# Moving the pools in SBUF by 192 bytes, so that the main matmul operands begin at multiples of 512 bytes

## The chip, the cores and the metric

The kernel runs on one core of one Trainium2 chip. The metric is the device time of one execution in microseconds. A trace by the hardware profiler shows one profiled execution; its span runs from the first to the last instruction of the program.

## What is computed

A trunk of four layers over x with 256 tokens of 1024 channels, float32. Each layer has a token mixer and then a SwiGLU network (FFN); after each of the two there is a residual sum and a layer norm. Cut to what matters:

```python
for i in range(4):
    kind = i % 3
    if kind == 0:   h = _hgrn2_mixer(x, ...)   # x @ w_in (1024 x 4096), gated recurrence, @ w_out (1024 x 1024)
    elif kind == 1: h = _mlstm_mixer(x, ...)   # x @ w_in (1024 x 3088), matrix memory, @ w_out (1024 x 1024)
    else:           h = _s5_mixer(x, ...)      # x @ w_in (1024 x 1024), state space, @ w_out (1024 x 2048)
    x = _layernorm(ALPHA * x + h, ...)
    x = _layernorm(ALPHA * x + _swiglu(x, w_gate_up[i], w_down[i]), ...)

def _swiglu(x, w_gate_up, w_down):             # 1024 x 5632 and 2816 x 1024
    gate, up = jnp.split(x @ w_gate_up, 2, axis=-1)
    return (jax.nn.silu(gate) * up) @ w_down
```

Layers 0 and 3 have the HGRN mixer, layer 1 the mLSTM mixer, layer 2 the S5 mixer.

## The kernel before

**Products in three parts.** The large products run on TensorE in the type float32r, in one pass. To keep float32's accuracy, each operand is split in two: hi, a copy of it in float32r, and lo, the rest. A product is then three matmuls, hi by hi, lo by hi and hi by lo, which add up in one bank of PSUM (`mm3`, L180 to L182).

**Weights.** They come from HBM in units of 128 partitions x 2048 float32 (1 MB). `fetch` (L101) loads a unit into a tile w of the pool `stage`, which has three buffers. `stage_next` (L112) splits each half of it into a pair of tiles hi and lo of 128 x 1024: ScalarE copies w to hi (L149), VectorE subtracts (L150). The pool `split` has 8 buffers for hi and 8 for lo. A plan (`plan`, L1361) gives the order of the units; `wstage` takes a unit and stages up to one unit ahead (`AHEAD`). SyncE (SP) issues the transfers, in the order that the scheduler gives them.

**The activation.** x is kept transposed and split in the tile xx, 128 partitions x 8 x 2 x 256: for each of eight blocks of channels, 256 tokens of the high part (`xh`) and 256 of the low one (`xl`). The layer norm writes it by way of TensorE's transposes (L271), which use the identity in the tile ident, and `put_split` (L290 and L291).

**Who is moving, who is stationary.** In a matmul the stationary operand (128 x 128, 512 bytes for each partition) is loaded first; the moving operand streams past it.
- `as_part` (L184): xx is stationary, the weights' hi and lo move, 512 columns. The rows of the profile are named g<-hi,xx and a<-hi,xx: output, moving, stationary.
- `ws_block` (L197): the weights are stationary, xx moves, 256 columns (g<-xx,hi).
- `ws_wide` (L205), in the FFN: hi stationary with xh and xl together moving, 512 columns (L210), and lo stationary with xh moving, 256 columns (L213).
- The FFN's second product: the hidden values, split in tiles hh and hl of 128 x 256, are stationary, the weights move, 512 columns (a<-hi,hh). The output projection of the mixers has the tiles oh and ol in the same role.

**The FFN's order.** For each block of 256 hidden channels: `across` makes the gate and the up values (L350 and L351 add the two halves of a bank), `parts` splits their product into hh and hl (L339, L340), `dproj` multiplies the block before.

**Memory.** SBUF is given out per partition, pool after pool and tile after tile, in the order in which they are made, each tile rounded up to 32 bytes. What the runtime and the framework keep ends at byte 16512 (32 times 512 and 128 more). Then follow the pool `const` (ident 512 bytes, root 32, eps 4, xx 16384, and later the two hnw of 4 bytes and lb of 64), `stage` (3 x 8192), `split` (16 x 4096), `xp` (3 x 4096), `gbp` (8192) and `small` (1216 in all). Every pool that a layer opens for itself lies behind these. In layer 0 and layer 1 the FFN's pool stands behind other tiles that live through it, those of the S5 preparation; those are at their place until the S5 mixer of layer 2 has ended.

**The small tiles.** root holds -0.5, for the powers on GpSimd (POOL) in `rsqrt` (L223). eps is the bias of one square root at the end. lb holds the lower bounds of the HGRN gates, written once in layer 1 (L480, L481) and read by ScalarE in layer 3. hnw0 and hnw1 are the norm weights of the two HGRN layers, loaded by SP (L589).

Of the kernel before, what the change touches and what calls it, by code (L numbers as in the profile page):

```python
# [9 lines left out]
F32 = mybir.dt.float32  # L10
# [7 lines left out]
P = 128  # L18
# [4 lines left out]
HEADS = 8  # L23
# [11 lines left out]
class Trunk:  # L35
    def __init__(self, ctx, tc, aps):
        self.ctx, self.tc, self.nc, self.a = ctx, tc, tc.nc, aps
        mk = lambda name, bufs, **kw: ctx.enter_context(tc.tile_pool(name=name, bufs=bufs, **kw))
        self.const = mk("const", 1)
        self.stage = mk("stage", 3)  # L40
        self.split = mk("split", 8)
        self.xp = mk("xp", 3)
        self.gbp = mk("gbp", 1)
        self.small = mk("small", 4)
        self.ps = mk("ps", 2, space=bass.MemoryType.PSUM)
        self.dram = mk("dram", 1, space=bass.MemoryType.DRAM)
        self.n = 0
        c = self.const
        self.ident = c.tile([P, P], F32, name="ident")
        self.root = c.tile([P, 8], F32, name="root")  # L50
        self.nc.gpsimd.memset(self.root, -0.5)
        self.eps = c.tile([P, 1], F32, name="eps")
        self.nc.gpsimd.memset(self.eps, LN_EPS)
        self.xx = c.tile([P, KD, 2, S], F32R, name="xx")
        self.xh, self.xl = (self.xx[:, :, i] for i in range(2))
        self.x = [None, None]
        self.lb = None
        self.tabled, self.loaded, self.table_name = [], None, None
        self.plan, self.ready, self.staged, self.taken = [], {}, 0, 0
        self.fetched, self.landed = 0, {}  # L60
        self.behind = None
# [393 lines left out]
    def lower_bounds(self):  # L455

        nc = self.nc
        t = self.const.tile([P, 2, HEADS], F32, name="lb")
        lp = self.lbp
        lg = lp.tile([P, DEPTH, HEADS], F32, name="lg")  # L460
        nc.sync.dma_start(lg, self.a["lb"])
        m = lp.tile([P, HEADS], F32, name="lbm")
        s = lp.tile([P, HEADS], F32, name="lbs")
        nc.vector.tensor_tensor(m, lg[:, 0, :], lg[:, 1, :], ALU.max)
        for l in range(2, DEPTH):
            nc.vector.tensor_tensor(m, m, lg[:, l, :], ALU.max)
        for l in range(DEPTH):
            nc.vector.tensor_tensor(lg[:, l, :], lg[:, l, :], m, ALU.subtract)
        self.act(lg, lg, AF.Exp)
        nc.vector.tensor_tensor(s, lg[:, 0, :], lg[:, 1, :], ALU.add)  # L470
        for l in range(2, DEPTH):
            nc.vector.tensor_tensor(s, s, lg[:, l, :], ALU.add)
        nc.vector.reciprocal(s, s)
        for l in range(DEPTH):
            nc.vector.tensor_tensor(lg[:, l, :], lg[:, l, :], s, ALU.mult)
        c = m
        nc.vector.tensor_tensor(c, lg[:, 0, :], lg[:, 1, :], ALU.add)
        for l in range(2, DEPTH):
            nc.vector.tensor_tensor(c, c, lg[:, l, :], ALU.add)
        nc.vector.tensor_tensor(t[:, 0, :], c, lg[:, 0, :], ALU.subtract)  # L480
        nc.vector.tensor_scalar(t[:, 1, :], t[:, 0, :], -1.0, 1.0, ALU.mult, ALU.add)  # L481
        return t

    def hgrn(self, j, gb, lb=None):

        nc, tc = self.nc, self.tc
        nw = self.const.tile([P, 1], F32, name=f"hnw{j}")
        with tc.tile_pool(name=self.uid("hg"), bufs=1, reuse_waits="tile") as hp, \
                tc.tile_pool(name=self.uid("hw"), bufs=2, reuse_waits="tile") as wp:
            msk = hp.tile([P, len(MASKED) + 1, 64], F32, name=self.uid("msk"))  # L490
# [1026 lines left out]
```

## Time and profile before

| | |
|---|---|
| median of three runs | 1255.83 us (1254.95 to 1257.53) |
| span of the profiled execution | 1251.8 us |
| matmuls on TensorE (PE), busy | 1234.0 us, 8464 instructions |
| weight loads on TensorE (PEld) | 1031.2 us, 8464 instructions |
| VectorE (DVE) | 957.8 us |
| ScalarE (ACT) | 694.6 us |
| GpSimd (POOL) | 34.7 us |
| read from HBM | 233.94 MB |

The three runs above are timed without the profile, and the profiled execution has no time of its own beside its span; the difference of the median to the span is 4.0 us. A row of the groups reads: line, engine, operation, output<-inputs, shape, count | busy us, mean ns of one | idle us of the engine ahead of them and who ended it. A matmul's duration has its fill time in it, which overlaps the next one. Where groups are asked for in a stretch of the span, they hold the instructions of that stretch alone. A row of stretches reads: from:to, length, and for PE, PEld and DVE (and others, if they are in it) busy us and count, then the granted clock, the DMA engines' share and GB/s.

### The profile page before, as it was taken

The page shows a single profiled execution, that of the slowest core. Times are in us where ns is not written, and L with a number is a line of the kernel's source. Part 1 is how long each engine was busy: PE and PEld are TensorE (multiplying, and loading weights), DVE is VectorE, ACT ScalarE, POOL GpSimd, SP SyncE. Part 2 cuts the span into 40 slices and gives each one's busy share as a digit, 9 for nine tenths or more (in the row PEclk, how much of TensorE's full clock was granted, in tenths as well). Part 3 has the DMA queues.
Part 4 walks back from the last instruction along what each step waited for, and adds up shares of the span by engine and source line. Part 5 has one row for each costly group of instructions (what it writes and reads, how often), then busy time and mean ns, then how long its engine had stood idle before and what let it go on. Part 6 is the DMA issues. An engine that isn't in the chain of part 4 may idle for free.

```text
span 1251.8 us, 21395 instructions
## 1 busy us (share of the span) xinstructions
PE 1234.0 (99%) x8464; PEld 1031.2 (82%) x8464; DVE 957.8 (77%) x1717; ACT 694.6 (55%) x1126; POOL 34.7 (3%) x60
## 2 busy tenths in 40 slices
PE   9999999999999999999998999999999999999997
PEld 7977788888788888888877788888889777888886
DVE  6887889796787799787599786666486887766664
ACT  6755575565467555555444355555359653555551
POOL 0000100000100100000000000000000000000000
PEclk9999999999999999999999999999999999999999
DMA  8733476666373278667556456555456433755530
GB/s 316 298 136 136 148 269 231 213 223 225 109 288 135 102 281 306 235 243 247 218 202 222 169 193 244 189 183 200 168 179 218 154 132 105 266 189 181 197 140 34
DMA packets 50245, 247.91 MB, mean 198 GB/s; under 512 B 6337, under 2 KB 15953, under 8 KB 23777
## 3 DMA queue, kind: packets, MB, share of 16 engines
q1 hardware_dynamic: 50016, 246.46, 54.7%
q8 instruction: 66, 1.08, 0.3%
q14 instruction: 35, 0.28, 0.1%
q0 software_dynamic: 128, 0.09, 0.0%
HBM read 233.94 MB, written 12.58 MB: 197 GB/s over the span
## 4 chain that ended last, share of the span: by engine, by line
PE 90%; DVE 5%; DMA 2%; ACT 2%; issue 0%; SPq 0%; DVEq 0%; ACTq 0%
PE g L210 18%; PE g L180 10%; PE g L182 10%; PE g L181 10%; PE g L213 9%; PE a L180 9%; PE a L181 8%; PE a L182 8%; DVE lo L150 1%; PE a L369 1%; PE t L271 1%; PE a L663 1%; DMA bc<-in_s_bc 1%; PE a L543 1%; DVE s5rot L1217 1%; DMA first<-in_first 1%
## 5 line engine op out<-in xcount | busy, mean ns | idle before, releaser
L150 DVE TENSOR_TENSOR lo<-w,hi 128x1024 fp32r<-128x1024 f32 x388 | 471.2, 1222 | 117.3 <-ACT hi L149 109.9
L149 ACT CAST hi<-w 128x1024 fp32r<-128x1024 f32 x388 | 405.5, 1051 | 187.5 <-PE a L181 100.6
L210 PE MATMUL g<-xx,hi 128*128 128x512 f32 x1024 | 356.7, 394 | 0.4 <-DVE sum L351 0.3
L213 PE MATMUL g<-xx,lo 128*128 128x256 f32 x1024 | 267.2, 281 | 0.0
L210 PEld LDWEIGHTS g<-xx,hi 128*128 128x128 f32 x1024 | 186.3, 188 | 36.1 <-DVE sum L351 1.1
L213 PEld LDWEIGHTS g<-xx,lo 128*128 128x128 f32 x1024 | 192.4, 188 | 11.0
L180 PE MATMUL g<-hi,xx 128*128 128x512 f32 (+1 forms) x416 | 167.5, 404 | 2.5 <-ACT xx L290 2.1
L182 PE MATMUL g<-lo,xx 128*128 128x512 f32 (+1 forms) x416 | 165.2, 399 | 0.1
L181 PE MATMUL g<-hi,xx 128*128 128x512 f32 (+1 forms) x416 | 164.6, 397 | 0.0
L180 PE MATMUL a<-hi,hh 128*128 128x512 f32 x328 | 129.5, 395 | 0.0
L350 ACT COPY sum<-g 128x256 f32<-128x256 f32 x128 | 47.7, 373 | 147.1 <-PE g L210 147.0
L182 PE MATMUL a<-lo,hh 128*128 128x512 f32 x328 | 129.1, 394 | 0.0
L181 PE MATMUL a<-hi,hl 128*128 128x512 f32 x328 | 128.9, 393 | 0.0
L351 DVE TENSOR_TENSOR sum<-g,sum 128x256 f32<-128x256 f32 x128 | 54.2, 423 | 63.5 <-ACT sum L350 62.9
L180 PEld LDWEIGHTS g<-hi,xx 128*128 128x128 f32 x416 | 78.3, 188 | 21.0 <-ACT xx L290 3.5
L182 PEld LDWEIGHTS g<-lo,xx 128*128 128x128 f32 x416 | 78.2, 188 | 18.2 <-DVE lo L150 1.4
L181 PEld LDWEIGHTS g<-hi,xx 128*128 128x128 f32 x416 | 78.4, 188 | 15.8
L182 PEld LDWEIGHTS a<-lo,hh 128*128 128x128 f32 x328 | 61.5, 188 | 14.5
L181 PEld LDWEIGHTS a<-hi,hl 128*128 128x128 f32 x328 | 61.5, 188 | 14.4 <-DVE hl L340 0.3
L180 PEld LDWEIGHTS a<-hi,hh 128*128 128x128 f32 x328 | 61.5, 188 | 12.6 <-ACT hh L339 0.2
L180 PE MATMUL g<-xx,hi 128*128 128x256 f32 x192 | 54.5, 284 | 0.0
L182 PE MATMUL g<-xx,hi 128*128 128x256 f32 x192 | 54.3, 283 | 0.0
(307 smaller groups left out, 1730.4 us busy)
## 6 DMA issues: line engine op xcount, KB each, us to landing
w<-in_w_gu SPq DMA_DIRECT2D x88, 1024.0 KB
w<-in_w_dn SPq DMA_DIRECT2D x44, 1024.0 KB
w<-in_w_hg SPq DMA_DIRECT2D x30, 1024.0 KB
w<-in_w_ml SPq DMA_DIRECT2D x12, 1024.0 KB
gb<-in_ln SPq DMA_DIRECT2D x8, 1024.0 KB
w<-in_w_ho SPq DMA_DIRECT2D x8, 1024.0 KB
w<-in_w_so SPq DMA_DIRECT2D x8, 1024.0 KB
w<-in_w_mo SPq DMA_DIRECT2D x4, 1024.0 KB
```

Source lines behind the costliest of these rows:

```text
L149: self.nc.scalar.copy(hi, x)
L150: i = self.nc.vector.tensor_tensor(lo, x, hi.bitcast(F32), ALU.subtract).ins
L180: mm(ps, lh, rh, start=start, stop=False)
L181: mm(ps, ll, rh, start=False, stop=False)
L182: mm(ps, lh, rl, start=False, stop=stop)
L210: whole = lambda: mm(ps, hi[:, c], self.xx[:, k].rearrange("p i t -> p (i t)"), start=k == 0, stop=k == KD - 1)
L213: mm(ps[:, S:], lo[:, c], self.xh[:, k], start=False, stop=False)
L271: nc.tensor.transpose(pt[:, (k % 4) * P : (k % 4 + 1) * P], z[:, k * P : (k + 1) * P], self.ident)
L350: nc.scalar.copy(t, ps[:, S:])
L351: nc.vector.tensor_tensor(t, ps[:, 0:S], t, ALU.add)
L369: nc.tensor.matmul(down[h][n], hidden(h, j, b)[x], dn[j][b][y][:, f], start=False, stop=(x, y, b) == steps[-1])
L543: nc.tensor.matmul(o, att[:, 2 * h + hd % 2, :], v[:, h, c], start=True, stop=h == 0)
```

## The change

The tiles root, eps, lb and the two hnw become slices of one tile, odds, of 384 bytes for each partition; it is made first, and ident is made behind xx. No instruction of the computation is added or taken away, and no shape is changed. The pool `const` is 192 bytes larger than before, and everything behind it begins 192 bytes later; xx begins 192 bytes earlier.

```diff
         c = self.const
-        self.ident = c.tile([P, P], F32, name="ident")
-        self.root = c.tile([P, 8], F32, name="root")
+        odds = c.tile([P, 96], F32, name="odds")
+        self.root, self.eps, self.bounds = odds[:, 0:8], odds[:, 8:9], odds[:, 16:32]
+        self.head_w = [odds[:, 32 + i : 33 + i] for i in range(2)]
         self.nc.gpsimd.memset(self.root, -0.5)
-        self.eps = c.tile([P, 1], F32, name="eps")
         self.nc.gpsimd.memset(self.eps, LN_EPS)
         self.xx = c.tile([P, KD, 2, S], F32R, name="xx")
+        self.ident = c.tile([P, P], F32, name="ident")
...
     def lower_bounds(self):
-        t = self.const.tile([P, 2, HEADS], F32, name="lb")
+        t = self.bounds.rearrange("p (a h) -> p a h", a=2)
...
     def hgrn(self, j, gb, lb=None):
-        nw = self.const.tile([P, 1], F32, name=f"hnw{j}")
+        nw = self.head_w[j]
```

## The prediction

> **What bounds the kernel now.** I read the page's busy shares first, then the list of waits of PE, then PE's groups by shape, and then the same groups in single stretches of the span.
>
> ```profile
> span 1251.8 us, 21395 instructions
> PE 1234.0 (99%) x8464; PEld 1031.2 (82%) x8464; DVE 957.8 (77%) x1717; ACT 694.6 (55%) x1126; POOL 34.7 (3%) x60
> PEclk9999999999999999999999999999999999999999
> q1 hardware_dynamic: 50016, 246.46, 54.7%
> ```
>
> TensorE is busy for 99% of the span at its full granted clock, VectorE for 77%, and the transfers fill 54.7% of the DMA engines. PE's own list of waits opens with these rows (total, times, longest):
>
> ```profile
> PE t L1247 <- issue: 2.2, 3, 0.8
> PE g L180 <- ACT xx L290: 2.1, 4, 0.7
> PE a L181 <- ACT xx L93: 1.7, 1, 1.7
> ```
>
> The longest total is 2.2 us, and no row names a DMA. So the time is a sum of matmuls standing back to back. Only what alters the time of one matmul moves it by more than a few us. The groups by shape:
>
> ```profile
> L210 PE MATMUL g<-xx,hi 128*128 128x512 f32 x1024 | 356.7, 394 | 0.4 <-DVE sum L351 0.3
> L213 PE MATMUL g<-xx,lo 128*128 128x256 f32 x1024 | 267.2, 281 | 0.0
> L181 PE MATMUL g<-hi,xx 128*128 128x512 f32 x408 | 162.2, 398 | 0.0
> L181 PE MATMUL a<-hi,hl 128*128 128x512 f32 x328 | 128.9, 393 | 0.0
> L181 PE MATMUL g<-xx,lo 128*128 128x256 f32 x192 | 54.0, 281 | 0.0
> L181 PE MATMUL a<-xx,lo 128*128 128x256 f32 x128 | 36.0, 281 | 0.0
> L181 PE MATMUL a<-hi,xx 128*128 128x512 f32 x64 | 25.6, 401 | 1.8 <-ACT xx L93 1.7
> L181 PE MATMUL a<-hi,ol 128*128 128x512 f32 x48 | 19.6, 408 | 0.0
> L369 PE MATMUL a<-hi,hl 128*128 128x512 f32 x24 | 7.7, 400 | 0.0
> ```
>
> The name after the arrow is the moving operand, the last one the stationary operand. Each L181 row stands for three, since L180 and L182 have the same counts; L369 likewise; the row with ol has a twin on the banks g. The 512-wide matmuls are 1024 + 3 x (408 + 328 + 64 + 48 + 48 + 24) = 3784; the 256-wide ones 1024 + 3 x (192 + 128) = 1984. A duration holds a fill time that overlaps the next matmul, so what counts is how much it differs from another one: 1 ns off each 512-wide matmul is 3.8 us, off each 256-wide one 2.0 us.
>
> **The change, part by part.** First, what moves. Adding up the sizes of the tiles in the order of their pools gives each address; I write it as the rest after 512 bytes. xx goes from 192 to 0, w, hi, lo, x and gb from 320 to 0. Everything behind them moves 192 bytes as well. hh and hl of the FFN stand behind other tiles in each layer: at 288 in layer 0, 128 in layer 1, and 0 in layers 2 and 3; they go to 480, 320 and 192. oh and ol, and v, att, k and q of the HGRN layers, go from 0 to 192. So the change aligns the common operands and takes the alignment from some that have it.
>
> The kernel before therefore holds an experiment of its own: the same three matmuls with hh and hl as stationary operand, whose moving operand never changes its address, with hh at 128 in layer 1 (467 to 590 us) and at 0 in layer 2 (757 to 890 us). Layer 1, then layer 2:
>
> ```profile
> L210 PE MATMUL g<-xx,hi 128*128 128x512 f32 x224 | 77.9, 394 | 0.0
> L182 PE MATMUL a<-lo,hh 128*128 128x512 f32 x61 | 24.1, 394 | 0.0
> L181 PE MATMUL a<-hi,hl 128*128 128x512 f32 x61 | 24.0, 394 | 0.0
> L180 PE MATMUL a<-hi,hh 128*128 128x512 f32 x61 | 24.0, 394 | 0.0
> ...
> L210 PE MATMUL g<-xx,hi 128*128 128x512 f32 x253 | 87.8, 394 | 0.0
> L180 PE MATMUL a<-hi,hh 128*128 128x512 f32 x64 | 25.2, 394 | 0.0
> L182 PE MATMUL a<-lo,hh 128*128 128x512 f32 x64 | 25.1, 392 | 0.0
> L181 PE MATMUL a<-hi,hl 128*128 128x512 f32 x64 | 24.9, 390 | 0.0
> ```
>
> L210, whose tiles lie at one place in all layers, stays at 394. The three with hh fall from 394 to (394 + 392 + 390) / 3 = 392. The matmuls with hl alone, in all four layers:
>
> ```profile
> 166.00:300.00 134.00, 25.29 (x64) 12.00 (x64) 6.56 (x16) 1.00 0.66 235
> 467.00:590.00 123.00, 24.05 (x61) 11.42 (x61) 6.99 (x18) 1.00 0.75 261
> 757.00:890.00 133.00, 24.94 (x64) 12.01 (x64) 6.96 (x17) 1.00 0.53 192
> 1070.00:1215.00 145.00, 24.94 (x64) 12.02 (x64) 7.70 (x19) 1.00 0.56 201
> ```
>
> The first pair of numbers is PE: 25.29 / 64 = 395 ns and 24.05 / 61 = 394 against 390 and 390. The step follows hh's address and not the order of the layers in time. So a stationary operand at a multiple of 512 is worth 2 ns for each matmul, and a multiple of 128 (layer 1) does not suffice. The issue times say the same: nine matmuls from 470.96 to 473.07 us are 234 ns each in layer 1, and nine from 841.06 to 843.13 us are 230 ns each in layer 2.
>
> ```profile
> 470.96 0.40 PE L182 MATMUL a<-lo,hh 128*128 128x512 f32 x1
> 473.07 0.39 PE L182 MATMUL a<-lo,hh 128*128 128x512 f32 x1
> 841.06 0.40 PE L180 MATMUL a<-hi,hh 128*128 128x512 f32 x1
> 843.13 0.39 PE L180 MATMUL a<-hi,hh 128*128 128x512 f32 x1
> ```
>
> That is between 2 and 4 ns; I take 2.5.
>
> 1. Stationary operand becomes aligned, 512-wide matmul: xx in 3 x (408 + 64) = 1416 and hi in 1024, together 2440 x 2.5 = -6.1 us (ends -4.9 and -9.8).
> 2. The same for 256-wide matmuls, 1984 of them: no row shows it. Between 0 and the 512-wide price, -5.0 us; I take half, -2.5.
> 3. Stationary operand loses its alignment: hh and hl of layers 2 and 3, half of 3 x (328 + 24) = 528 matmuls, and oh and ol, 3 x (48 + 48) = 288: 816 x 2.5 = +2.0 us (ends +1.6 and +3.3).
> 4. Moving operand becomes aligned: all 3784 and 1984. No matmul of these groups has an aligned moving operand, so this is unknown. A loss isn't excluded (first rival below). For the gain, the far end is a stream that loses nothing. L810 multiplies float32, where 256 columns take the cycles of 512:
>
> ```profile
> L810 PE MATMUL a<-qz,ky x16: 378/379/470, 383.3 to 399.0; 128*128 128x256 f32 x16
> L545 PE MATMUL a<-v,cross 128*128 128x128 f32 x32 | 6.2, 275 | 0.0
> ```
>
> The median of 379 against L210's 394 gives 15 ns, and 275 (128 columns of float32, the cycles of 256) against 281 gives 6: 3784 x 15 + 1984 x 6 = 69 us less as the end. The near row is item 1's: a moving row of 2 KB begun off a multiple of 512 touches one such block more, as a stationary row does. At 2.5 ns that would be -9.5 us and, halved for 256 columns, -2.5 more. Since what made the stationary row slow isn't shown to act on the moving one, I take half of 12: -6 us.
> 5. VectorE and ScalarE: L351 takes 423 ns in layer 1 and 425 in layer 2, the other way round and by 2 ns, and neither engine ends PE's waits. Nothing; PE's work covers it, and with that cover gone it is 128 x 2 ns = 0.3 us.
>
> ```profile
> L351 DVE TENSOR_TENSOR sum<-g,sum 128x256 f32<-128x256 f32 x28 | 11.8, 423 | 8.5 <-ACT sum L350 8.4
> ...
> L351 DVE TENSOR_TENSOR sum<-g,sum 128x256 f32<-128x256 f32 x31 | 13.2, 425 | 20.8 <-ACT sum L350 20.8
> ```
>
> 6. One tile, odds, in place of root, eps, lb and two hnw. If waits are kept by tile, the second hnw transfer, which SP issues at 55.5 us today, must come behind ScalarE's last reading of lb at 968.7 us, and weight fetches queue behind it on SP; the next pow on POOL waits for it to land. If they are kept by region, nothing changes.
>
> ```profile
> L589 SPq DMA_DIRECT2D hnw<-in_hg_nw x2: 426/832/1237, 22.5 to 55.5; - x2
> L93 ACT ACTIVATE k<-k,lb x8: 493/494/495, 946.6 to 968.7; 128x256 f32<-128x256 f32 x8
> num<-in_c_caus POOLq DMA_DIRECT2D x1, 64.0 KB, 2.3
> ```
>
> The price is 0 to one small landing, 2.3 us; I take 0, since weights are fetched a unit ahead.
>
> Sum: -6.1 - 2.5 + 2.0 - 6 = -12.6 us. The profiled execution spans 1251.8 us and the median of the three runs is 1255.8, so 4.0 us lie outside the span and stay: 1239.2 + 4.0 = 1243.2, about 1243.
>
> **The rivals.**
>
> *Distance, not place; slower.* Stationary and moving rows are read side by side, so what counts could be their distance within 512: with hi at 320 it was 32, 192, 320 and 320 in layers 0 to 3, and both shift together, so hh would change nothing. xx and hi stand 128 apart today and 0 afterwards. The nearest shown distance, 32 (layer 0), has the slowest row, 395. If rows begun at the same place hinder each other by 4 ns, the size of the known step with its sign turned, the 2440 matmuls of item 1 cost +9.8 us: 1265.6. It decides from 1 ns on. Against it: nothing shows that equality is worse than 32 or 192.
>
> *No difference.* The steps in hh may come from a pattern of issue that also depends on neighbours, and the gain of item 1 may be eaten by items 3 and 4. Rows begun 64 past 128 and rows begun at 512 hold as many pieces of 16 bytes, and were this the unit, no address here would matter: 1255.8. The Trainium skill gives this unit, in "SBUF — State Buffer", Specifications: lines of 16 bytes. By that page the change does nothing. This case's trace disagrees as far as hh goes: 394 against 390 for places that are both multiples of 16.
>
> *The whole loss goes.* If misplaced moving rows are all that separates 394 from 379, the end of item 4 comes: 1255.8 - 69 + 2 = 1189; half of it is 1222. The Trainium skill, "TensorE: Matmul & The Clock Gate", section "Wait — 56ns, not 53.3ns?", gives 215.7 ns from start to start for 512 columns; by that figure, an estimate, the 230 to 234 ns seen here have 14 to 18 to lose. Against it: an aligned stationary row won 2 to 4.
>
> **How the numbers follow.** Alignment pays in the sizes above, 1232 to 1252: 0.56. The whole or half of the loss goes, below 1230: 0.08. No difference, within 0.2% (2.5 us, about what a measurement of this kernel can tell): 0.18. Slower: 0.18. The forecast is 1243 us. The range from 1222 to 1262 leaves out the far ends of the gain (0.05) and of the loss (0.10). The likeliest case's own range is 1232 to 1252. Of its 0.56 a little lies within 2.5 us of no change; faster 0.63, same 0.19, slower 0.18.
>
> **What the new profile would show.** L210 at 394 and L181 with xx fall by 2 to 4 ns (item 1), more if the moving operand counts (item 4). hl of layers 2 and 3 rises from 390 to about 394 under my reading, stays under the rival of distance, and falls everywhere if the moving operand rules. L213 stays within 281 and 278. DVE and ACT rows stay. The prediction is wrong if L210 goes above 394, if PE gets waits on SP or POOL above 3 us, or if its durations fall towards 380.

## The result and the profile after

The kernel with the change takes 1251.28 us (median of 7 runs, 1250.03 to 1252.51) against 1255.05 us before (1254.04 to 1257.53). The ratio is 0.9967, with a 95% interval from 0.9956 to 0.9978: 0.33% faster, about 3.8 us where 12.6 were forecast. The span went from 1251.8 to 1248.4 us. All lines stand one lower in the file, so L210 is now L211 and L180 to L182 are L181 to L183.

The page after, its head and the busy shares, and the first rows of PE's list of waits (us in total, times, longest):

```profile
span 1248.4 us, 21395 instructions
PE 1228.9 (98%) x8464; PEld 1030.2 (83%) x8464; DVE 957.0 (77%) x1717; ACT 694.1 (56%) x1126; POOL 34.7 (3%) x60
PEclk9999999999999999999999999999999999999999
q1 hardware_dynamic: 50016, 246.46, 54.9%
...
PE t L1248 <- issue: 3.5, 3, 1.7
PE g L181 <- ACT xx L291: 2.0, 4, 0.7
PE a L182 <- ACT xx L94: 1.8, 1, 1.8
```

PE is busy 5.1 us less (1234.0 to 1228.9), and the span is only 3.4 us shorter: PE's idle time rose from 17.8 to 19.5 us. The granted clock, the other engines and the transfers are what they were. The gain lies inside the matmuls, so their groups by shape come next:

```profile
L211 PE MATMUL g<-xx,hi 128*128 128x512 f32 x1024 | 356.4, 397 | 0.4 <-DVE sum L352 0.3
L214 PE MATMUL g<-xx,lo 128*128 128x256 f32 x1024 | 264.9, 279 | 0.0
L182 PE MATMUL g<-hi,xx 128*128 128x512 f32 x408 | 160.8, 395 | 0.0
L182 PE MATMUL a<-hi,hl 128*128 128x512 f32 x328 | 129.5, 395 | 0.0
L182 PE MATMUL g<-xx,lo 128*128 128x256 f32 x192 | 54.4, 283 | 0.0
L182 PE MATMUL a<-xx,lo 128*128 128x256 f32 x128 | 36.2, 283 | 0.0
L182 PE MATMUL a<-hi,xx 128*128 128x512 f32 x64 | 25.4, 397 | 2.0 <-ACT xx L94 1.8
```

The groups answer with different signs. The as_part matmuls with xx stationary fell by 3 to 4 ns (398 to 395, 401 to 397). The moving 512 of `ws_wide` rose from 394 to 397 and its partner of 256 columns fell from 281 to 279. The 256-wide matmuls of `ws_block` rose from 281 to 283. The hidden values, of which layers 2 and 3 should have lost, stand at 395 after 393.

Durations overlap, so the sum has to be taken over the times from one start to the next. Between the same two starts of an unbroken sequence of 31 as_part matmuls, before and then after:

```profile
142.38 0.40 PE L180 MATMUL g<-hi,xx 128*128 128x512 f32 x1
149.60 0.39 PE L181 MATMUL g<-hi,xx 128*128 128x512 f32 x1
```

```profile
142.41 0.39 PE L181 MATMUL g<-hi,xx 128*128 128x512 f32 x1
149.44 0.39 PE L182 MATMUL g<-hi,xx 128*128 128x512 f32 x1
```

7.22 us divided by 31 is 233 ns, and 7.03 by 31 is 227. PE issues the same sequence of matmuls in both kernels, so every one can be paired with itself. Grouped, with times over 245 ns cut off there so that waits don't enter (my working on the start times of the two traces):

| group | matmuls | start to start before, ns | after | us |
|---|---|---|---|---|
| xx stationary, 512 wide (as_part) | 1416 | 233.8 | 230.5 | -4.7 |
| hi stationary, 512 wide (L210/L211, with 8 of the gates) | 1032 | 231.3 | 233.7 | +2.4 |
| lo stationary, 256 wide (L213/L214) | 1024 | 119.0 | 115.9 | -3.1 |
| xx moving, 256 wide (ws_block) | 960 | 120.6 | 121.3 | +0.7 |
| hh, hl stationary | 1055 | 231.7 | 231.5 | -0.2 |
| oh, ol stationary | 288 | 231.1 | 231.1 | 0.0 |
| everything else | 2688 | | | -0.3 |

Together that is -5.2 us, close to the 5.1 us by which the page's busy time of PE fell, and +1.8 us of times over 245 ns, close to the 1.7 us by which its idle time rose. The prediction's price for the place of an operand, a gain wherever one becomes aligned, doesn't give groups of both signs. Before the change xx and hi stood 128 bytes apart within 512, afterwards 0; hh kept its distance from hi. (From here on a distance is the address of the moving operand less that of the stationary one.) So two theories stand against each other from here. *Place*: each operand has a price by its own address. *Distance*: what counts is how far apart the moving and the stationary operand begin, counted within some power of two.

### The profile page after: what moved, and what is told of

Its sections match the earlier page's. It is cut to its first block, busy times and chain, and to the rows that moved or that the text cites. A ratio compares the mean times of both kernels' runs of the same rounds, so it can differ in the third digit from the quotient of the medians.

```text
span 1248.4 us, 21395 instructions
## 1 busy us (share of the span) xinstructions
PE 1228.9 (98%) x8464; PEld 1030.2 (83%) x8464; DVE 957.0 (77%) x1717; ACT 694.1 (56%) x1126; POOL 34.7 (3%) x60
## 4 chain that ended last, share of the span: by engine, by line
PE 89%; DVE 5%; DMA 2%; ACT 2%; issue 1%; SPq 0%; DVEq 0%; POOL 0%; ACTq 0%
PE g L211 18%; PE g L181 10%; PE g L183 10%; PE g L182 10%; PE g L214 9%; PE a L182 8%; PE a L181 8%; PE a L183 8%; DVE lo L151 1%; PE a L370 1%; PE t L272 1%; DMA bc<-in_s_bc 1%; PE a L664 1%; DMA first<-in_first 1%; PE a L544 1%; DVE s5rot L1218 1%
## 5 line engine op out<-in xcount | busy, mean ns | idle before, releaser
L211 PE MATMUL g<-xx,hi 128*128 128x512 f32 x1024 | 356.4, 397 | 0.4 <-DVE sum L352 0.3
L214 PE MATMUL g<-xx,lo 128*128 128x256 f32 x1024 | 264.9, 279 | 0.0
L211 PEld LDWEIGHTS g<-xx,hi 128*128 128x128 f32 x1024 | 186.0, 188 | 37.1 <-DVE sum L352 1.1
L214 PEld LDWEIGHTS g<-xx,lo 128*128 128x128 f32 x1024 | 193.2, 189 | 10.9
L181 PE MATMUL g<-hi,xx 128*128 128x512 f32 (+1 forms) x416 | 166.3, 401 | 3.0 <-ACT xx L291 2.0
L183 PE MATMUL g<-lo,xx 128*128 128x512 f32 (+1 forms) x416 | 164.0, 396 | 0.1
L182 PE MATMUL g<-hi,xx 128*128 128x512 f32 (+1 forms) x416 | 163.2, 393 | 0.0
L182 PE MATMUL a<-hi,hl 128*128 128x512 f32 x328 | 129.5, 395 | 0.0
L183 PE MATMUL a<-lo,hh 128*128 128x512 f32 x328 | 129.4, 395 | 0.0
L181 PE MATMUL a<-hi,hh 128*128 128x512 f32 x328 | 129.0, 394 | 0.0
L352 DVE TENSOR_TENSOR sum<-g,sum 128x256 f32<-128x256 f32 x128 | 54.1, 423 | 61.8 <-ACT sum L351 61.3
L181 PEld LDWEIGHTS g<-hi,xx 128*128 128x128 f32 x416 | 78.2, 188 | 20.0 <-ACT xx L291 3.5
L183 PEld LDWEIGHTS g<-lo,xx 128*128 128x128 f32 x416 | 78.1, 188 | 17.5 <-DVE lo L151 1.9
L182 PEld LDWEIGHTS g<-hi,xx 128*128 128x128 f32 x416 | 78.3, 188 | 14.6
L182 PEld LDWEIGHTS a<-hi,hl 128*128 128x128 f32 x328 | 61.6, 188 | 14.6 <-DVE hl L341 0.5
L183 PEld LDWEIGHTS a<-lo,hh 128*128 128x128 f32 x328 | 61.7, 188 | 13.5
L181 PEld LDWEIGHTS a<-hi,hh 128*128 128x128 f32 x328 | 61.6, 188 | 13.1 <-ACT hh L340 0.5
L181 PE MATMUL g<-xx,hi 128*128 128x256 f32 x192 | 54.5, 284 | 0.0
L183 PE MATMUL g<-xx,hi 128*128 128x256 f32 x192 | 54.5, 284 | 0.0
```

What stands on the lines that cost most here:

```text
L181: mm(ps, lh, rh, start=start, stop=False)
L182: mm(ps, ll, rh, start=False, stop=False)
L183: mm(ps, lh, rl, start=False, stop=stop)
L211: whole = lambda: mm(ps, hi[:, c], self.xx[:, k].rearrange("p i t -> p (i t)"), start=k == 0, stop=k == KD - 1)
L214: mm(ps[:, S:], lo[:, c], self.xh[:, k], start=False, stop=False)
L352: nc.vector.tensor_tensor(t, ps[:, 0:S], t, ALU.add)
```

## The experiments

**A map of distances.** Only matmuls, of tiles that lie still in SBUF; of the trunk nothing is computed. 64 matmuls stand in each group, d and n with the stationary operand at a multiple of 512 and the moving one so many bytes further (512 and 256 columns), m with both widths in turn, s with both operands 64 bytes further on. The map and the patterns further down were executed once each.

```diff
+        for d in range(0, 512, 32):
+            run(f"d{d:03d}x", (512,), 0, d)
+        for d in (0, 64, 128, 192, 256, 320, 384, 448):
+            run(f"s{d:03d}x", (512,), 64, d)
...
+        for d in range(0, 512, 32):
+            run(f"n{d:03d}x", (256,), 0, d)
+        for d in range(0, 512, 32):
+            run(f"m{d:03d}x", (512, 256), 0, d)
```

> This kernel leaves out the whole trunk and copies x to the output; it only runs float32r matmuls without any waits, in groups of 64, moving operand from one tile and stationary operand from another, eight stationary slices in turn. Groups named d000x to d480x: 512 columns, the stationary slices at multiples of 512 bytes, the moving slices so many bytes past one. s000x to s448x: the same distances, both 64 bytes later. f: one pair of slices again and again, with whole multiples of 512 added. n: 256 columns. m: 512 and 256 columns in turn. Distance: the durations differ by group d, lowest near 0 and 320, 4 to 6 ns higher at 32, 128 and 192, and group s repeats group d within 1 ns. Place: d000x is the lowest, all other d are equal within 1 ns, and s000x is 3 to 5 ns above d000x. No difference by address: all of d and s within 1 ns.

The groups by shape (busy us, mean ns of one), those that decide:

```profile
L35 PE MATMUL d000x<-mov,sta 128*128 128x512 f32 x64 | 14.7, 389 | 0.0
L35 PE MATMUL d032x<-mov,sta 128*128 128x512 f32 x64 | 15.1, 395 | 0.0
L35 PE MATMUL d064x<-mov,sta 128*128 128x512 f32 x64 | 14.8, 391 | 0.0
L35 PE MATMUL d128x<-mov,sta 128*128 128x512 f32 x64 | 15.1, 395 | 0.0
L35 PE MATMUL d192x<-mov,sta 128*128 128x512 f32 x64 | 15.1, 396 | 0.0
L35 PE MATMUL d256x<-mov,sta 128*128 128x512 f32 x64 | 14.7, 389 | 0.0
L35 PE MATMUL d320x<-mov,sta 128*128 128x512 f32 x64 | 14.8, 391 | 0.0
L35 PE MATMUL s000x<-mov,sta 128*128 128x512 f32 x64 | 14.7, 389 | 0.0
L35 PE MATMUL s128x<-mov,sta 128*128 128x512 f32 x64 | 15.0, 394 | 0.0
L35 PE MATMUL n000x<-mov,sta 128*128 128x256 f32 x64 | 7.8, 283 | 0.0
L35 PE MATMUL n128x<-mov,sta 128*128 128x256 f32 x64 | 7.8, 282 | 0.0
L35 PE MATMUL n192x<-mov,sta 128*128 128x256 f32 x64 | 7.4, 276 | 0.0
```

Read down d: 0 and 256 take 389, 64 and 320 take 391, everything else 395 or 396. The pattern repeats after 256 bytes, not 512. The s rows have the stationary operand 64 bytes off every multiple of 128, and repeat the d rows within 2 ns: s000 is 389, s128 is 394. So distance counts here, and place does not. From start to start that is 226.7 ns at distance 0 against 233.2 at 128, 229.1 at 64. For 256 columns it is another curve: 0 is among the slowest (283) and 192 the quickest (276). The m groups repeat after 256 bytes too, with one exception that stays unexplained: a pair of 512 and 256 columns takes 346.8 ns from start to start at distance 0 and 353.2 at 256. The map also fits the row on which the prediction was built. hh stood 32, 192, 320 and 320 bytes from hi in the four layers, and the map gives 395, 396, 391 and 391 where the trace of before had 395, 394, 390 and 390 (hl).

**The whole layout 64 bytes earlier.** All distances are as in the changed kernel, and no common operand is at a multiple of 128 any more.

```diff
-        odds = c.tile([P, 96], F32, name="odds")
+        odds = c.tile([P, 80], F32, name="odds")
```

> The changed kernel with odds 64 bytes shorter, so that xx, w, hi and lo all begin 64 bytes short of a multiple of 512 (448), hh and hl at 416, 256, 128 and 128. No distance between any two of them is changed. Distance: 1251.3 us as with the change, within 1.5 us, and the same step in the group with hh between the first two layers and the last two. Place: the gain is gone, 1255 us.

1251.06 us, ratio to before 0.9972 (0.9962 to 0.9983): the changed kernel's gain, with none of the alignment of its common operands. By tile (shortest, median and longest duration), two rows of this kernel and, below them, the second one's counterpart of before:

```profile
L211 PE MATMUL g<-xx,hi x1024: 387/395/504, 171.4 to 1213.5; 128*128 128x512 f32 x171
L182 PE MATMUL g<-hi,xx x416: 278/389/506, 5.7 to 1235.4; 128*128 128x512 f32 x137, 128*128 128x256 f32 x2
...
L181 PE MATMUL g<-hi,xx x416: 274/393/508, 5.4 to 1238.0; 128*128 128x512 f32 x137, 128*128 128x256 f32 x2
```

The matmuls with xx stationary have a median of 389, where before had 393. Paired start to start, no group of the table above differs by more than 0.2 us from the changed kernel. The step in the group with hh stays as well: leaving out times over 245 ns, a matmul takes 233 ns in the first two layers and 229 in the last two. Place is refuted, for stationary and moving operand at once.

**The distance of 128 put back.** xx goes to 384 within 512; weights, x and the FFN's tiles stay where the change put them.

```diff
-        odds = c.tile([P, 96], F32, name="odds")
+        odds = c.tile([P, 64], F32, name="odds")
...
         self.ident = c.tile([P, P], F32, name="ident")
+        c.tile([P, 32], F32, name="rest")
```

> The changed kernel with xx at 384 (behind 256 bytes of odds) and the other 128 bytes behind ident: w, hi, lo, hh and hl lie exactly as with the change, only xx goes back to the distance that it had before (hi - xx = 128). Distance: the rows with xx go back to before, 3 to 4 ns more for a 512-wide matmul with xx stationary, L211 2.4 ns less, L214 3 ns more; 1254.5 to 1255.5 us. Place: xx is at a multiple of 128 but not of 512, the weights stay at multiples of 512, so that most of the gain stays: 1251 to 1253 us.

1255.05 us, ratio 1.0007 (0.9998 to 1.0016): the whole gain is gone, though the staged and split weights are still at multiples of 512.

```profile
L212 PE MATMUL g<-xx,hi x1024: 387/396/502, 172.3 to 1216.4; 128*128 128x512 f32 x171
L215 PE MATMUL g<-xx,lo x1024: 274/281/287, 172.5 to 1216.3; 128*128 128x256 f32 x171
L183 PE MATMUL g<-hi,xx x416: 274/393/508, 5.5 to 1238.6; 128*128 128x512 f32 x137, 128*128 128x256 f32 x2
```

Paired as above against the changed kernel: xx stationary +4.7 us, L211's matmuls -2.4, L214's +3.1, ws_block -0.7. Each group goes back by what it had moved.

**Distance 0 for the hidden values.** A pad in the FFN's pool puts hh and hl 0 bytes from hi (within 256) in all four layers.

```diff
             down = [[self.bank("a") for _ in range(2)] for _ in range(2)]
+            fp.tile([P, (8, 48, 80, 80)[i]], F32, name=self.uid("pad"), bufs=1)
```

> The changed kernel with a tile of 32, 192, 320 and 320 bytes ahead of the FFN's own tiles, so that hh and hl lie at multiples of 512 in all four layers, at distance 0 from the weights. Distance: the matmuls with hh fall by 4 to 5 ns each in the first two layers (528 of them, -2.4 us) and stay within 1 ns in the last two: 1249 us. Place: they fall in all four layers, 2.5 ns each, -2.6 us: 1248.7 us, the last two layers included.

1248.15 us, ratio 0.9945 (0.9932 to 0.9958), 3.1 us below the changed kernel. Its row with hl, and the changed kernel's:

```profile
L182 PE MATMUL a<-hi,hl x328: 388/389/504, 165.5 to 1235.6; 128*128 128x512 f32 x164
```

```profile
L182 PE MATMUL a<-hi,hl x328: 388/393/503, 166.5 to 1237.6; 128*128 128x512 f32 x164
```

The median falls from 393 to the map's 389, and paired start to start the hh group gives 4.1 us: 5.7 ns a matmul in the first two layers (-3.0 us) and 2.1 ns in the last two (-1.1 us). So the expectation under distance missed: the last two layers were to stay within 1 ns. The total of 1248.15 us alone speaks no more for distance than for place, whose 1248.7 us is the nearer. The split decides: place has one price for all layers, while the map has 6.7 ns from distance 32 or 192 to 0 and 2.4 from 64 to 0. In the two profiled executions 1.6 us of the gain came back as times over 245 ns, 1.1 of them at L211.

**The kernel's own patterns, and two controls.** Again matmuls alone: the orders of as_part (p), ws_wide (w) and ws_block (b) over real distances, then a stationary operand that alternates between distance 0 and 128, then plain float32, where each of the kernel's matmuls stands twice in the trace, as two passes.

```diff
+        for x, h, l in ((0, 0, 0), (192, 320, 320), (0, 64, 0), (0, 64, 64), (0, 0, 64), (0, 192, 0), (0, 0, 192), (0, 64, 128)):
+            name = f"{x:03d}_{h:03d}_{l:03d}x"
+            parts(name, x, h, l)
+            wide(name, x, h, l)
+            block(name, x, h, l)
+        turns("evenx", "oddx", 0)
+        for d in (0, 32, 64, 128, 192):
+            slow(f"full{d:03d}x", d)
```

> The three matmul patterns of the kernel run alone, with no DMA beside them; the rest of the trunk is left out. Name pAAA_BBB_CCCx: the three-product order with the x pair stationary (512 wide); w...: pairs of one 512-wide and one 256-wide matmul with the weights stationary; b...: the three-product order with the weights stationary (256 wide). AAA, BBB and CCC are the places in bytes, modulo 256, of x, of the upper and of the lower weights. Theory (the distance of moving from stationary operand, modulo 256, sets the rate): p000_000_000x 389 ns a matmul and 227 start to start, p192_320_320x 395 and 233; with hi or lo alone at 64, two thirds or one third of p falls to 391. The w pairs come out at 347 to 353 ns in all of them, so within 2%. The b pattern is quickest where the distance x minus weights is 192, that is with the weights at 64. Rival (place, each operand by itself): 000_064_064 would cost all of the p pattern's gain. Alternating stationary tiles (evenx, oddx: the even ones at distance 0 and the odd ones at 128 from one moving tile): if a matmul's own stationary tile counts, evenx 389 and oddx 395; if the tile that is loaded beside it counts, the other way round. Full fp32 (names fullAAAx): passes run at a quarter of the rate, so the theory expects no dependence on distance, within 1%.

Here each stretch is one pattern of 96 (p, b) or 64 (w) matmuls; the count in brackets has those that reach in from outside. The stretches are p at (0, 0, 0), the layout after; p at (192, 320, 320), the layout before; p at (0, 64, 64); then w after, w before, b after, b before; last, p at (0, 64, 0), (0, 0, 64) and (0, 0, 192):

```profile
37.75:59.51 21.76, 21.76 (x97) 1.00 0.00 0
82.20:104.52 22.32, 22.32 (x99) 1.00 0.00 0
171.91:194.31 22.40, 22.40 (x98) 1.00 0.00 0
59.51:70.70 11.19, 11.19 (x66) 1.00 0.01 1
104.52:115.71 11.19, 11.19 (x65) 1.00 0.01 1
70.70:82.20 11.50, 11.50 (x97) 1.00 0.01 1
115.71:127.11 11.40, 11.40 (x98) 1.00 0.01 1
...
127.11:149.49 22.38, 22.38 (x98) 1.00 0.00 0
216.87:239.14 22.27, 22.27 (x98) 1.00 0.00 0
306.41:328.40 21.99, 21.99 (x98) 1.00 0.00 0
```

The as_part order takes 226.7 ns for each matmul in the layout after and 232.5 in the one before; ws_wide takes 174.8 in both; ws_block 119.8 against 118.7, so the change costs it 1 ns. These are the three signs of the kernel's table (-3.3, about 0 over the pair, +0.7) without a DMA or another engine at work.

Several expectations missed. The w pairs spread by 2.4% (171.8 to 175.9 ns for each matmul), not within 2%. ws_block isn't quickest with the weights at 64; all layouts measured with hi or lo 64 or 192 off lay between 117.7 and 118.2. And what p does off distance 0 isn't what the map gives for each matmul by itself. At (0, 64, 64) it takes 233.3 ns and not 229, which the expectation had named as the sign of place. With hi alone at 64 it takes 233.1, with lo alone 232.0, where a share of the gain should have stayed; lo alone at 192 costs less (229.1) than at 64, the other way round from the map. Place is no way out, since the kernel shifted by 64 bytes and the s rows of the map have it refuted. Nor is it the three-product order as such: in the trunk, hh of the last two layers stands at distance 64 modulo 256 in the same order and takes 229 ns. So distance 0 for every matmul is shown to be quickest in this order, and the map doesn't predict its time at 64 or where distances are mixed. The controls:

```profile
L74 PE MATMUL oddx<-xx,hi 128*128 128x512 f32 x32 | 12.7, 396 | 0.0
L72 PE MATMUL evenx<-xx,hi 128*128 128x512 f32 x32 | 12.6, 395 | 0.0
...
L79 PE MATMUL full000x<-whole 128*128 128x256 f32 x64 | 14.1, 380 | 0.0
L79 PE MATMUL full128x<-whole 128*128 128x256 f32 x64 | 14.0, 379 | 0.0
```

With every other stationary tile off, even and odd are both slow, so one neighbour off is enough, and the test doesn't tell whether a matmul's own tile or the one loaded beside it counts. The passes of plain float32, 215.8 ns from start to start for 256 columns (217.0 in the first group), show no dependence on distance.

**Distance 0 for all as_part matmuls.** The FFN pads, and 64 bytes ahead of oh and ol.

```diff
     def transposed(self, pool):
+        pool.tile([P, 16], F32, name=self.uid("pad"))
```

> The changed kernel with the pads in the FFN pools that put hh and hl at distance 0 in all four layers, and 64 bytes more in front of oh and ol, so that all 512-wide matmuls with streamed weights have distance 0. Distance theory: 288 matmuls with oh or ol stationary go from 395 to 389, so 0.7 to 1.7 us under the kernel with the FFN pads alone (1248.15): 1247.0, range 1246.0 to 1248.5. Place theory: no change from the changed kernel, 1251.3.

1246.85 us (1243.59 to 1247.91), ratio 0.9929 (0.9917 to 0.9942): the fastest of all, 4.4 us below the changed kernel. The row with ol, and the changed kernel's:

```profile
L182 PE MATMUL g<-hi,ol x48: 387/389/458, 117.6 to 1041.4; 128*128 128x512 f32 x48
```

```profile
L182 PE MATMUL g<-hi,ol x48: 387/393/467, 118.2 to 1043.8; 128*128 128x512 f32 x48
```

The median falls to the map's 389. But the part of oh and ol is small: paired start to start against the changed kernel 0.25 us, where 0.7 to 1.7 had been expected. The upper end was reckoned from 395, while oh and ol had stood at distance 64, where the map has 391. That the total came out at 1246.85, next to the expected 1247.0, is chance so far as oh and ol go. The 1.3 us between the medians of this kernel and the one with FFN pads alone lie in intervals that overlap, so what the second pad adds to the time is not settled.

## Why the prediction was wrong

It forecast 12.6 us less, and 3.8 were measured: the direction came out, the mechanism and the size did not.

*What bounds the kernel* held: a few ns for each matmul moved the time. The waits, the only other part that moved, took 1.8 us back.

*The reading of hh* is the step that failed, and items 1 to 4 rest on it. The step from 394 to 390 between layer 1 and layer 2 is real, but hh's address and its distance from hi changed together there, and the prediction took the address: it put 2.5 ns on a stationary operand at a multiple of 512. The runs show a price of the distance in its place, 6.6 ns between 128 and 0 for 512 columns, and none of the address. (That the step follows the address and not the order in time was not shown either: 395, 394, 390, 390 fall in order of time too. It is settled by the pads, with which the matmuls of all four layers take 227 ns.) Its own rival named the distance, listed the right four numbers, and said that a common shift of both would then leave hh as it is. It did, start to start: the pairing gives hh and hl -0.2 us in all. The durations of hl mislead here, as they overlap; they rose from 393 to 395 as a whole, in all layers and not in the last two alone.

*Item 1, xx stationary* (1416 x 2.5 = -3.5): measured -4.7 us. Right in sign and nearly in size, and that is luck: the distance became 0 by the same shift that aligned the place.

*Item 1, hi stationary in L210* (1024 x 2.5 = -2.6): measured +2.4 us. The sign is wrong, and L210's row at 397, above 394, is one of the signs that the prediction had named for being wrong. In `ws_wide` this matmul alternates with one of 256 columns, and what the one lost the other won.

*Item 2, 256-wide* (-2.5): measured -3.1 + 0.7 = -2.4 us, but as two halves with opposite signs. L214's gain belongs to L211's loss, and the pair as a whole gained 0.7 us. ws_block, which the price had been guessed for, lost. The agreement of the sum is chance.

*Item 3, alignment taken from hh, hl, oh and ol* (+2.0): measured -0.3 us for hh and hl in layers 2 and 3, and 0.0 for oh and ol. There was no alignment to lose.

*Item 4, the moving operand's place* (-6): 0. The kernel 64 bytes earlier shows it, since no common operand there is aligned and no group is slower than with the change by more than 0.1 us. This term was half of a price that no row showed, and it alone is 6 us of the 7.4 between -12.6 and -5.2 us of matmuls; items 1 and 3 nearly cancel (+5.0 for L210, -1.2 for xx, -2.2 for item 3, with hh and hl of all four layers).

*Items 5 and 6* (0): right. L352 keeps its median of 425 ns, and the second small load, now into odds, is issued at 55.8 us as it was at 55.5:

```profile
L590 SPq DMA_DIRECT2D odds<-in_hg_nw x2: 426/782/1138, 22.8 to 55.8; - x2
```

*The rest of the gap*, from 5.2 us of matmuls to 3.4 of span, is 1.8 us of waits. The row `PE t L1248 <- issue` rose from 2.2 to 3.5 us in the profiled executions. The other pages speak for waits that follow from faster matmuls, one execution each: PE's idle time is 17.8 and 17.9 us in the two kernels with xx and hi at distance 128 (before, and the distance put back), and 18.8 to 20.2 us in the four at distance 0. What these waits wait for was not tested.

*The rivals.* Distance was the right mechanism with the wrong sign: equal starts are the best case for 512 columns, not the worst. Its remark that nothing shows equality as worse than 32 or 192 was the better guide. No difference is refuted: the map has 6 ns between distance 0 and 32, both multiples of 16 bytes. The Trainium skill, "SBUF — State Buffer", Specifications, gives lines of 16 bytes; by these lines alone all the addresses are alike, and the map disagrees by those 6 ns. The whole loss did not go: after the change the steady as_part sequence still takes 227 ns from start to start.

## What to carry to other kernels

When an address looks as if it mattered, write down for each row the place of both operands and their difference, and look for a shift that keeps the one and changes the other; here one kernel shifted by 64 bytes, and one with the old distance put back, settled it. A term with no row behind it deserves its own experiment or a small number: half of a guessed price was the largest part of this miss. Where moving tiles of 512 columns in float32r stand back to back, pads of 32 to 320 bytes that put stationary and moving operands a multiple of 256 bytes apart are worth trying, per pair and not per tile; here, with the change, they took 0.7% off (ratio 0.9929).

## What the chip showed that was not expected

- Where float32r matmuls of 512 columns repeat at one distance of moving and stationary operand within a partition, their time depends on it modulo 256 bytes: about 227 ns from start to start at 0, 229 at 64, 232 to 234 at the other distances tried. In the three-product order run alone, 64 and mixed distances don't take the times of this map (233.3 at 64).
- So where the stationary operand lies is not indifferent to the moving operand's stream: their distance alone is worth 6.6 ns of 233. The Trainium skill, "TensorE: Matmul & The Clock Gate", section "Step-by-step: what each phase is for", has two independent read ports for them and says that loading the next tile's weights doesn't steal read bandwidth from the running matmul. The map has 6.6 ns that don't fit two reads independent of each other; that it is bandwidth which is lost is not shown.
- With 256 columns the order is another: 113.4 ns at 192, 117.4 to 119.9 elsewhere. A distance that is best for the one shape is poor for the other; in alternation the two nearly cancel.
- The passes of plain float32 (379 or 380 ns at all five distances) don't show it.
- Why a distance of 64 helps in the map and in the trunk (229 ns from start to start) and not in the patterns run alone (233.3), and whether the own or the next stationary tile is the partner, stays open, as does the cause in the memory itself: no run here looked inside it.
